# A decoder block on one core: the first weights in two parts, the compressed key's norm joined to another, 18 routing constants

## The chip, the core and the metric

The kernel runs on one core of a Trainium2 chip. A core has TensorE (PE in the rows: matmuls and transposes, with PEld for loading the stationary operand), VectorE (DVE), ScalarE (ACT), GpSimd (POOL) and SyncE (SP), which here only issues loads and stores. The metric is the device time of one execution in microseconds (us); smaller is better. The time before is the median of three runs.

## The reference

One block of a decoder for 512 tokens of width 2048 in float32. Cut to what matters here:

```python
h = rms(x, attn_norm_g);  proj = h @ w_in            # q, 6 x k/v, branch gates, pool input, merge gates
kc = rope(rms(compress(k_cmp), k_norm_cmp_g));  vc = compress(v_cmp)
    # compress: blocks of 32 tokens + position embedding, silu(flat @ w1) @ w2
q, k_slc, k_swa = rope(rms(., gain)) each
o = gate0*attend(q, kc, vc) + gate1*attend(selected blocks) + gate2*attend(window)
y = merge0 * (o @ w_head_out) + merge1 * (pool(pool_in) @ w_pool) * pool_scale
x = x + y @ w_out
p = softmax(rms(x) @ w_router_group + b), top group;  top 2 of its 4 experts
x = x + sum of the chosen experts' (silu(h @ w_gate) * (h @ w_up)) @ w_down
```

## The kernel before

Every large product is done three times over in a split form: a weight piece is loaded (`raw_*`), ScalarE casts it to its high part (`hi_*`), VectorE or GpSimd subtracts the two to get the low part (`lo_*`), and TensorE multiplies high by high, low by high and high by low (`mm3`, lines 133 to 136; `Piece.split`, lines 173 to 197). Which of the two engines subtracts is a pattern of letters for each kind of weight in `PLAN['lo']`: G is GpSimd, V VectorE, read in a circle.

`run` (line 201) walks over a list of such pieces in a fixed order. The string `PLAN['main']` sets the order of the second stage: after the eight pieces `cmp` of the compressed keys and values come two gate pieces (g, h), then pieces of the first attention group's queries, keys and values (q; q0, q2, ... q14), mixed with four pieces K0 to K3 of the compression's first weights for the keys and V0 to V3 for the values (called `w` in tile names; their product is `H`). A second string, `PLAN['side']`, is a row of slots, one taken after each part of a piece; a letter is a function that runs there, a dot an empty slot. `g` is the gate's transposes (`gate_T`, line 571), `B` and `D` build the compression's input from the transposed keys and values (`Xf`, its high part `Xh`, its low part `Xl`, lines 459 to 463), `h` and `i` transpose the hidden layer `cth` into `hsT` (line 492) and copy it with a factor (line 498), `k` makes the compressed key with its norm and rope (`cmp_key`, lines 505 to 526), `w` transposes that key (`kcT`, line 530) and makes the compressed value (`c2v`, line 537), `v` is the latter alone. The queue of each engine keeps the order in which the program records its instructions.

**The opening.** x is loaded in column pieces, transposed on TensorE (`ht`, line 402), multiplied by the norm's gain `gcol` into its high part by ScalarE (line 403) and its low part by VectorE (line 404); the first `cmp` piece is loaded, cast and subtracted whole. `gcol` itself comes from a transpose (`gcolp`, line 309).

**The first attention group's queries and keys.** When q14 is through, VectorE works along a chain (lines 618 to 642): squares, an inverse root over 24 columns, norm, gains, rope. TensorE transposes the result (`qT`, line 658). The same chain runs for groups 1 to 3, later.

**The routing.** The last product with `w_out` ends token tile by token tile; each tile is added to x, squared with a sum on ScalarE (line 1048), transposed (`xgT`, line 1081), copied by ScalarE (`xgt`, line 1083) and multiplied by the router's weights (`lgp`, line 1088). Small operations on VectorE follow (from `lg`, line 1420, to `mx`, line 1451), then a product with constants (`pref`, line 1457). In between, `warm_up` (line 1412) lets TensorE multiply constants whose result nobody reads.

Of the kernel before, what the change touches and what calls it, by code (L numbers as in the profile page):

```python
# [76 lines left out]
def hybrid_block_kernel(  # L77
# [262 lines left out]
    def late_loads():  # L340
        q = nc.sync
        for i in range(4):
            q.dma_start(gain[:, i], q_norm_g.to_broadcast([128, 64]))
        q.dma_start(gain[:, 4], k_norm_slc_g.to_broadcast([128, 64]))
        q.dma_start(gain[:, 5], k_norm_swa_g.to_broadcast([128, 64]))
# [156 lines left out]
    kc_row = early.tile([128, 64], F32, name="kc_row")  # L502
    kcd = early.tile([128, 2, 64], F32, name="kcd")

    def cmp_key():
# [11 lines left out]
        rt = early.tile([128, 4, 8], F32, name="crt")  # L517
# [1079 lines left out]
```

## Time and profile before

| | before |
|---|---|
| median of 3 runs | 1443.61 us (1442.37 to 1444.62) |
| the profiled execution | 1442.58 us, its span 1440.8 us |
| mean granted clock of TensorE | 0.984 of full |
| TensorE busy | 1388.4 us, 96% |
| VectorE busy | 825.1 us, 57% |
| ScalarE busy | 765.6 us, 53% |
| GpSimd busy | 445.4 us, 31% |

Busy shares say which engine could be the bound. The list of waits says for what an engine stood idle, and for how long; the number in square brackets at the end of a timeline row is the same for one instruction. [...]

### The profile page before, as it was taken

The page shows a single profiled execution, that of the slowest core. Times are in us where ns is not written, and L with a number is a line of the kernel's source. Part 1 is how long each engine was busy: PE and PEld are TensorE (multiplying, and loading weights), DVE is VectorE, ACT ScalarE, POOL GpSimd, SP SyncE. Part 2 cuts the span into 40 slices and gives each one's busy share as a digit, 9 for nine tenths or more (in the row PEclk, how much of TensorE's full clock was granted, in tenths as well). Part 3 has the DMA queues.
Part 4 walks back from the last instruction along what each step waited for, and adds up shares of the span by engine and source line. Part 5 has one row for each costly group of instructions (what it writes and reads, how often), then busy time and mean ns, then how long its engine had stood idle before and what let it go on. Part 6 is the DMA issues. An engine that isn't in the chain of part 4 may idle for free.

```text
span 1440.8 us, 18395 instructions
## 1 busy us (share of the span) xinstructions
PE 1388.4 (96%) x6638; PEld 1138.2 (79%) x6638; DVE 825.1 (57%) x1258; ACT 765.6 (53%) x1289; POOL 445.4 (31%) x289
## 2 busy tenths in 40 slices
PE   8998999989999999999999999999999999999995
PEld 7877788778778788788888888888887777777774
DVE  4663773666463453555543202453255899999995
ACT  4543356564666465655665322332242687777784
POOL 0044342322333343243434455211021322222221
PEclk9999999999999999999999999999999999999998
DMA  6344233233333333343434453785675899999994
GB/s 224 94 115 123 80 102 87 77 107 85 91 116 111 92 93 87 96 117 97 109 110 125 117 141 108 224 326 166 226 252 175 279 362 367 367 358 354 330 363 84
DMA packets 193188, 249.88 MB, mean 173 GB/s; under 512 B 50384, under 2 KB 137536, under 8 KB 191264
## 3 DMA queue, kind: packets, MB, share of 16 engines
q1 hardware_dynamic: 176640, 199.13, 43.6%
q0 software_dynamic: 11808, 41.09, 10.0%
q10 hardware_dynamic: 4640, 8.40, 1.6%
q8 instruction: 54, 0.88, 0.3%
q14 instruction: 46, 0.38, 0.1%
HBM read 225.49 MB, written 35.65 MB: 181 GB/s over the span
## 4 chain that ended last, share of the span: by engine, by line
PE 79%; DVE 10%; ACT 6%; issue 2%; DMA 1%; POOL 1%; ACTq 0%; SPq 0%; POOLq 0%; DVEq 0%
PE z L134 7%; PE z L136 7%; PE z L135 7%; PE gu L136 4%; PE gu L134 4%; PE gu L135 4%; PE wo L134 4%; PE wo L136 4%; PE wo L135 4%; PE qkv L135 2%; PE qkv L134 2%; PE qkv L136 2%; PE dn L134 2%; PE dn L135 2%; PE dn L136 2%; PE xT L1245 2%
## 5 line engine op out<-in xcount | busy, mean ns | idle before, releaser
L197 POOL TENSOR_TENSOR lo_z<-raw_z,hi_z 128x1024 fp32r<-128x1024 f32 x64 | 153.4, 2401 | 200.5 <-ACT hi_z L196 192.8
L134 PE MATMUL z<-hT,hi_z 128*128 128x512 f32 x512 | 204.1, 399 | 0.0
L136 PE MATMUL z<-hT,lo_z 128*128 128x512 f32 x512 | 200.7, 392 | 0.0
L135 PE MATMUL z<-hT,hi_z 128*128 128x512 f32 x512 | 200.2, 391 | 0.0
L140 DVE TENSOR_TENSOR ptl<-pt,pth 128x512 fp32r<-128x512 f32 (+1 forms) x96 | 57.8, 602 | 177.0 <-ACT pth L139 176.8
L197 DVE TENSOR_TENSOR lo_gu<-raw_gu,hi_gu 128x2048 fp32r<-128x2048 f32 x64 | 146.8, 2294 | 9.8 <-ACT hi_gu L196 4.2
L196 ACT CAST hi_gu<-raw_gu 128x2048 fp32r<-128x2048 f32 x64 | 122.3, 1911 | 18.7 <-PE gu L136 9.9
L778 ACT ACTIVATE p<-s,m 128x128 f32<-128x128 f32 (+3 forms) x128 | 66.4, 523 | 115.6 <-DVE m L776 112.4
L197 POOL TENSOR_TENSOR lo_qkv<-raw_qkv,hi_qkv 128x1024 fp32r<-128x1024 f32 x28 | 70.6, 2521 | 173.8 <-ACT hi_qkv L196 148.6
L136 PEld LDWEIGHTS z<-hT,lo_z 128*128 128x128 f32 x512 | 96.5, 189 | 21.2
L135 PEld LDWEIGHTS z<-hT,hi_z 128*128 128x128 f32 x512 | 96.7, 189 | 18.6
L134 PEld LDWEIGHTS z<-hT,hi_z 128*128 128x128 f32 x512 | 96.9, 189 | 18.3
L134 PE MATMUL gu<-hi_gu,xh 128*112 128x512 f32 x256 | 106.4, 416 | 0.1
L134 PE MATMUL qkv<-hi_qkv,hT 128*128 128x512 f32 x256 | 103.5, 404 | 0.1
L135 PE MATMUL qkv<-lo_qkv,hT 128*128 128x512 f32 x256 | 101.4, 396 | 0.3 <-POOL lo_qkv L197 0.3
L136 PE MATMUL gu<-hi_gu,xl 128*112 128x512 f32 x256 | 101.7, 397 | 0.0
L136 PE MATMUL qkv<-hi_qkv,hT 128*128 128x512 f32 x256 | 101.5, 396 | 0.0
L134 PE MATMUL wo<-hi_wo,y 128*128 128x512 f32 x256 | 101.1, 395 | 0.0
L135 PE MATMUL gu<-lo_gu,xh 128*112 128x512 f32 x256 | 100.4, 392 | 0.0
L136 PE MATMUL wo<-hi_wo,y 128*128 128x512 f32 x256 | 99.8, 390 | 0.0
L135 PE MATMUL wo<-lo_wo,y 128*128 128x512 f32 x256 | 99.7, 389 | 0.0
L1313 POOL DMA_INDIRECT out_dram<-y,idx x18 | 60.1, 3337 | 107.7 <-ACT hi_gu L196 88.6
(419 smaller groups left out, 3193.7 us busy)
## 6 DMA issues: line engine op xcount, KB each, us to landing
raw_z<-in_w_in_dram SPq DMA_DIRECT2D x128, 256.0 KB
raw_gu<-in_w_expert_gate_dram SPq DMA_DIRECT2D x59, 512.0 KB
raw_gu<-in_w_expert_up_dram SPq DMA_DIRECT2D x59, 512.0 KB
raw_dn<-in_w_expert_down_dram SPq DMA_DIRECT2D x28, 1024.0 KB
raw_wo<-in_w_out_dram SPq DMA_DIRECT2D x32, 512.0 KB
raw_qkv<-in_w_in_dram SPq DMA_DIRECT2D x32, 256.0 KB
raw_qkv<-in_w_in_dram SPq DMA_DIRECT2D x128, 64.0 KB
raw_u<-in_w_in_dram SPq DMA_DIRECT2D x16, 512.0 KB
```

The lines of the kernel that those rows point to most:

```text
L134: T.matmul(ps, ah, bh, start=start, stop=False)
L135: T.matmul(ps, ah, bl, start=False, stop=False)
L136: T.matmul(ps, al, bh, start=False, stop=stop)
L140: V.tensor_tensor(lo, src, f(hi), op=OP.subtract)
L196: A.copy(self.hi[sl], self.raw[sl])
L197: self.eng.tensor_sub(self.lo[sl], self.raw[sl], f(self.hi[sl]))
L778: A.activation(p[:, b], v[:, b], AF.Exp, bias=m[:, b:b + 1], scale=0.125, accum_out=m[:, 2 + b:3 + b])
L1245: T.transpose(pt[:, j * RS:(j + 1) * RS], self.xr[:, k0 * 128 + j:(k0 + 4) * 128:4], ident[0:RS, 0:RS])
L1313: ins = G.indirect_dma_start(out=dst, out_offset=bass.IndirectOffsetOnAxis(ap=idx, axis=0), in_=src, in_offset=None, bounds_check=n - 1, o ...
```

## The change

**Opening.** The first `cmp` piece is loaded in two halves, one for each of its two rows of 128 inputs, and cast and subtracted in two cuts. It is no longer split ahead of everything, but behind the first two x tiles, so that on ScalarE the first x tile (`hh[0]`) stands ahead of the cast; the second (`hh[1]`) is made by VectorE. The splits of the next two pieces stand behind the x tiles 2 and 3. The gain's transpose goes into a bank of the constants' tile, so the first `ht` waits for nothing that reads it. The first twelve `cmp` matmuls run as four of high by high, four of low x, four of low weight.

**Slots and engines.** `g` moves three slots on, behind q4 and K1; `i` and the compressed value one slot on; the key's transpose leaves its slot. In `PLAN['lo']` two subtractions go from GpSimd to VectorE: K1's and q6's.

**The compressed key's norm.** The two operations for its sum of squares, its inverse root and the rest, 14 on VectorE, go: ScalarE squares the key with a sum (`kc_sum`), the sum becomes a 25th column of the first group's inverse root, and scaling and rope of the key run behind that group's rope, followed by its transpose.

**Gains.** The operation with the queries' and keys' gains, one of 1536 columns, becomes one of 4 x 256 and one of 4 x 128, and the tile of gains is loaded in three parts rather than six.

**Routing.** The transposes of the last two tiles are recorded ahead of what they stood behind, and 15 constants become 18.

```diff
-    'side': 'mnab.Bcd.gD.........h.k.iw',
+    'side': 'mnab.Bcd..D.g.......h.k..iv',
-    'lo': {'qkv': 'VGVGVGVGGG...', ..., 'w': 'GGV', ...},
+    'lo': {'qkv': 'VGVVVGVGGG...', ..., 'w': 'GVVGGVGG', ...},
...
-    pc = o_tile("gcolp")
-    T.transpose(pc[:, 0:16], grow, ident[0:16, 0:16])
-    V.tensor_copy(gcol, pc[:, 0:16])
+    T.transpose(warm[:, 1, 0:16], grow, ident[0:16, 0:16])
+    V.tensor_copy(gcol, warm[:, 1, 0:16])
+    cmp[0].cuts = tuple((slice(None), slice(k, k + 1)) for k in range(2))
+    cmp0_mm = cmp[0].mm
+    def cmp0_first(wh, wl, part):
+        if part:
+            return cmp0_mm(wh, wl, part)
+        cmp0.extend(mm_tile(f"cmp_{t}") for t in range(NT))
+        for i, (a, w) in enumerate(((hh[0], wh), (hl[0], wh), (hh[0], wl))):
+            for t in range(NT):
+                T.matmul(cmp0[t], a[:, t * 128:(t + 1) * 128], w[:, 0], start=i == 0, stop=False)
+    cmp[0].mm = cmp0_first
...
-            A.mul(hh[k], ps, gcol[:, k:k + 1])
+            if k == 1:
+                V.tensor_scalar(hh[k], ps, gcol[:, k:k + 1], None, op0=OP.mult)
+            else:
+                A.mul(hh[k], ps, gcol[:, k:k + 1])
...
         A.copy(kc_row, po[:, 0:64])
-        sq = early.tile([128, 64], F32, name="csq")
-        V.tensor_mul(sq, kc_row, kc_row)
-        cs = early.tile([128, 3], F32, name="cs")
-        V.tensor_reduce(cs[:, 0:1], sq, axis=AX.X, op=OP.add)
-        V.tensor_scalar(cs[:, 0:1], cs[:, 0:1], 1.0 / HD, EPS, op0=OP.mult, op1=OP.add)
-        rsqrt(cs[:, 1:2], cs[:, 0:1], cs[:, 2:3])
-        V.scalar_tensor_tensor(kc_row, kc_row, cs[:, 1:2], gainc, op0=OP.mult, op1=OP.mult)
+        A.activation(kcd[:, 0], po[:, 0:64], AF.Square, accum_out=kc_sum)
+    def cmp_key_rope(inverse):
+        V.scalar_tensor_tensor(kc_row, kc_row, inverse, gainc, op0=OP.mult, op1=OP.mult)
...
+            if g == 0:
+                V.tensor_copy(s2[:, NT * 6:], kc_sum)
...
-                V.tensor_tensor(q3, q3, gain.rearrange("p h d -> p (h d)")[:, None, :].to_broadcast([128, NT, 384]),
+                V.tensor_tensor(qn[:, :, 0:4], qn[:, :, 0:4], gain[:, 0, None, None, :].to_broadcast([128, NT, 4, 64]),
+                                op=OP.mult)
+                V.tensor_tensor(qn[:, :, 4:6], qn[:, :, 4:6], gain[:, None, 1:3].to_broadcast([128, NT, 2, 64]),
                                 op=OP.mult)
...
+            key = [lambda: cmp_key_rope(rs[:, NT * 6:])] if g == 0 else []
+            if g == 0:
+                deferred.append(cmp_keyT)
...
-            residual_tile(3, t, ps[t])
             if t:
                 router_T(3, t - 1)
+            residual_tile(3, t, ps[t])
...
-                tl[0] += [lambda: router_mm(3, 2), lambda: router_T(3, 3), lambda: router_mm(3, 3)]
+                tl[0] += [lambda: router_T(3, 3), lambda: router_mm(3, 2), lambda: router_mm(3, 3)]
...
-    cmp[0].split()
-    run(main, side)
+    run(main, side, split_lead=lambda i: 2 if i else 0)
...
-    warm_up(15)
+    warm_up(18)
```

VectorE's queue at the second half of the compression's input, before: `gates` reads the gate's transposes, `Xf` and `Xl` belong to the values, the `lo_w` behind them is K2's.

```order
L451 COPY kT_165<-kvT_799 64x511 x2
L572 TENSOR_SCALAR gates<-gateT 128x192
L459 TENSOR_TENSOR Xf_867<-kT_165,cols 128x2048
L463 TENSOR_TENSOR Xl_870<-Xf_867,Xh_869 128x2048
L197 TENSOR_TENSOR lo_w_888<-raw_w_885,hi_w_887 128x1024
```

The same place after:

```order
L469 COPY kT_168<-kvT_799 64x511 x2
L197 TENSOR_TENSOR lo_w_823<-raw_w_820,hi_w_822 128x1024
L197 TENSOR_TENSOR lo_qkv_6_846<-raw_qkv_6_839,hi_qkv_6_845 128x1024
L477 TENSOR_TENSOR Xf_861<-kT_168,cols 128x2048
L481 TENSOR_TENSOR Xl_864<-Xf_861,Xh_863 128x2048
L197 TENSOR_TENSOR lo_w_882<-raw_w_879,hi_w_881 128x1024
L585 TENSOR_SCALAR gates<-gateT 128x192
```

The subtractions of K1 (`lo_w_823`) and q6 now stand between the last key copy and `Xf`, and `gates` stands behind K2's subtraction.

TensorE's queue at the transposes of the values' hidden layer, before: `H` is the product with V3, `hi_qkv_12` and `lo_qkv_12` are q12's weights.

```order
L134 MATMUL H_961<-hi_w_1054,Xh_869 128x256
L135 MATMUL H_961<-lo_w_1055,Xh_869 128x256
L136 MATMUL H_961<-hi_w_1054,Xl_870 128x256
L492 MATMUL hsT_1158<-ident,cth_1155 128x128 x2
L134 MATMUL qkv_0_738<-hi_qkv_12_1117,hT_88 128x512
L135 MATMUL qkv_0_738<-lo_qkv_12_1118,hT_88 128x512
```

The same transposes after, with the end of the matmuls of q12's first part ahead of them:

```order
L134 MATMUL qkv_3_741<-hi_qkv_12_1093,hT_88 128x512
L135 MATMUL qkv_3_741<-lo_qkv_12_1094,hT_88 128x512
L136 MATMUL qkv_3_741<-hi_qkv_12_1093,hT_88 128x512
L510 MATMUL hsT_1152<-ident,cth_1131 128x128 x2
L134 MATMUL qkv_0_738<-hi_qkv_12_1093,hT_88 128x512
L135 MATMUL qkv_0_738<-lo_qkv_12_1094,hT_88 128x512
```

They have moved behind the twelve matmuls of q12's first part, and `c2v`, which read their copy behind that part, now stands behind the second.

TensorE's queue at the end of the routing's products, before:

```order
L1081 MATMUL xgT_2_9057<-ident,xg_2_9021 128x128 x4
L1088 MATMUL lgp<-wr_7643,xgt_1_9032 128x20 x4
L1088 MATMUL lgp<-wr_7643,xgt_2_9062 128x20 x4
L1081 MATMUL xgT_3_9072<-ident,xg_3_9051 128x128 x4
L1088 MATMUL lgp<-wr_7643,xgt_3_9077 128x20 x4
L1412 MATMUL warm_9097<-ones 128x512 x15
```

And after:

```order
L1100 MATMUL xgT_2_9040<-ident,xg_2_9018 128x128 x4
L1107 MATMUL lgp<-wr_7633,xgt_1_9015 128x20 x4
L1100 MATMUL xgT_3_9058<-ident,xg_3_9048 128x128 x4
L1107 MATMUL lgp<-wr_7633,xgt_2_9045 128x20 x4
L1107 MATMUL lgp<-wr_7633,xgt_3_9063 128x20 x4
L1430 MATMUL warm_9087<-ones 128x512 x18
```

The transposes of tile 3 have gone ahead of the product with tile 2, and three constants are added.

## Rows read from the trace of the kernel before

**Rows 1.** The page, part 1: each engine's busy us, share of the span, instructions.
```profile
PE 1388.4 (96%) x6638; PEld 1138.2 (79%) x6638; DVE 825.1 (57%) x1258; ACT 765.6 (53%) x1289; POOL 445.4 (31%) x289
```

**Rows 2.** List of TensorE's waits: waiting instruction, releaser, us in total, times, longest.
```profile
PE qT L658 <- DVE qn L642: 2.3, 1, 2.3
...
PE lgp L1088 <- ACT xgt L1083: 1.5, 2, 0.8
```

**Rows 3.** Timeline, opening: start, us, engine, line, operation, count, idle before and its releaser.
```profile
7.67 1.04 ACT L196 CAST hi_cmp<-raw_cmp 128x1024 fp32r<-128x1024 f32 x1 [4.91 <-DMA raw_cmp<-in_w_in_dram]
...
8.62 1.26 ACT L403 ACTIVATE hT<-ht,gcol 128x512 fp32r<-128x512 f32 x2
...
9.36 0.50 PE L134 MATMUL cmp<-hi_cmp,hT 128*128 128x512 f32 x1 [2.15 <-ACT hT L403]
...
9.89 1.40 DVE L404 SCALAR_TENSOR_TENSOR hT<-ht,gcol,hT 128x512 fp32r<-128x512 f32 x2
...
14.36 1.04 PE L402 MATMUL ht<-ident,xt 128*128 128x128 f32 x8
```

**Rows 4.** Stretch of the opening: busy time by engine, granted clock, DMA share, GB/s.
```profile
11.00:13.00 2.00, 2.00 (x6) 1.52 (x6) 1.52 (x2) 0.69 (x1) 0.00 (x0) 0.50 1.04 378
```

**Rows 5.** Timeline, gate to weight piece K2: TensorE, VectorE, GpSimd, ScalarE.
```profile
73.41 3.71 DVE L459 TENSOR_TENSOR Xf<-kT,cols 128x2048 f32<-128x2048 f32 x1
...
87.12 0.42 PE L571 MATMUL gateT<-ident,gt 48*128 48x48 f32 x4 [1.87 <-DVE kT L451]
...
87.85 5.37 DVE L459 TENSOR_TENSOR Xf<-kT,cols 128x2048 f32<-128x2048 f32 x1
...
88.08 1.05 ACT L196 CAST hi_qkv<-raw_qkv 128x1024 fp32r<-128x1024 f32 x1 [0.88 <-DMA raw_qkv<-in_w_in_dram]
...
96.10 0.40 PE L134 MATMUL qkv<-hi_qkv,hT 128*128 128x512 f32 x1
...
97.47 2.39 POOL L197 TENSOR_TENSOR lo_w<-raw_w,hi_w 128x1024 fp32r<-128x1024 f32 x1 [2.01 <-ACT hi_w L196]
...
97.53 3.42 DVE L197 TENSOR_TENSOR lo_w<-raw_w,hi_w 128x1024 fp32r<-128x1024 f32 x1
...
101.57 0.28 PE L134 MATMUL H<-hi_w,Xh 128*128 128x256 f32 x1
```

**Rows 6.** Stretch behind the gate's transposes, columns as in rows 4.
```profile
89.00:91.00 2.00, 2.00 (x6) 1.58 (x5) 2.00 (x1) 0.12 (x1) 2.00 (x2) 0.50 0.47 141
```

**Rows 7.** Timeline, compressed key and value: GpSimd, VectorE, TensorE, ScalarE.
```profile
122.21 2.34 POOL L197 TENSOR_TENSOR lo_qkv<-raw_qkv,hi_qkv 128x1024 fp32r<-128x1024 f32 x1 [3.47 <-ACT hi_qkv L196]
...
122.28 2.28 DVE L130 SCALAR_TENSOR_TENSOR cs<-cs 128x1 f32<-128x1 f32 x1
...
126.12 1.22 DVE L197 TENSOR_TENSOR lo_qkv<-raw_qkv,hi_qkv 128x1024 fp32r<-128x1024 f32 x1
...
127.73 0.69 PE L492 MATMUL hsT<-ident,cth 128*128 128x128 f32 x2 [5.38 <-DVE cth L481]
...
129.38 1.04 ACT L196 CAST hi_u<-raw_u 128x1024 fp32r<-128x1024 f32 x1
...
133.80 2.00 PE L537 MATMUL c2v<-w2v,hsTv 128*128 128x64 f32 x16 [0.38 <-DVE kcT L531]
```

**Rows 8.** Stretch behind `hsT`, columns as in rows 4.
```profile
127.00:132.00 5.00, 4.26 (x11) 3.46 (x12) 0.68 (x2) 1.96 (x2) 1.51 (x1) 0.50 0.51 151
```

**Rows 9.** The gains' line 629: times, least, median and longest ns, starts, forms.
```profile
L629 DVE TENSOR_TENSOR qn<-qn,gain x4: 1747/1754/3826, 156.9 to 614.2; 128x1536 f32<-128x1536 f32 x4
```

**Rows 10.** Timeline, routing: the constants, the choice's last operation, the prefix sums.
```profile
1107.43 6.04 PE L1412 MATMUL warm<-ones 128*128 128x512 f32 x15
...
1111.38 0.22 DVE L1451 TENSOR_TENSOR mx<-gs,top 128x64 fp32r<-128x64 f32 x1
...
1113.31 0.20 PE L1457 MATMUL pref<-mx,tri 128*128 128x80 f32 x1
```

**Rows 11.** Stretch of the routing constants, columns as in rows 4.
```profile
1106.00:1112.00 6.00, 6.00 (x19) 5.03 (x19) 3.89 (x25) 0.21 (x1) 0.00 (x0) 0.50 0.91 334
```

More of the change, by code (lines that the diff above doesn't have):

```diff
@@ L282, in hybrid_block_kernel @@
     invb = mix.tile([128, S], F32, name="invb")
-    rtmp = mix.tile([128, 24], F32, name="rtmp")
+    rtmp = mix.tile([128, 25], F32, name="rtmp")
+    kc_row = mix.tile([128, 64], F32, name="kc_row")
+    kcd = mix.tile([128, 2, 64], F32, name="kcd")
+    kc_sum = mix.tile([128, 1], F32, name="kc_sum")
+    gainc = mix.tile([128, 64], F32, name="gainc")
     gates = mix.tile([128, NT, 48], F32, name="gates")
@@ L295, in hybrid_block_kernel @@
     nc.scalar.dma_start(grow, attn_norm_g.rearrange("o (k p) -> (o k) p", p=128))
-    cmp = token_major("cmp", lambda raw, k0: [(raw, wcols(k0, 2, C_KC, 512))], hh, hl, lambda ps: cmp_done(ps), one=(KT - 2,),
+    cmp0 = []
+    cmp = token_major("cmp", lambda raw, k0: [(raw[:, k:k + 1], wcols(k0 + k, 1, C_KC, 512)) for k in range(2)]
+                      if k0 == 0 else [(raw, wcols(k0, 2, C_KC, 512))], hh, hl, lambda ps: cmp_done(ps), one=(KT - 2,), out=cmp0,
                       pre={4: lambda: load_x(2, 4), 8: lambda: load_x(4, 6),
@@ L320, in hybrid_block_kernel @@
     sc = mix.tile([128, 5, 2, 8], F32, name="sincos")
-    gain = mix.tile([128, 6, 64], F32, name="gain")
+    gain = mix.tile([128, 3, 64], F32, name="gain")
     posi = early.tile([128, 5], I32, name="posi")
-    gainc = early.tile([128, 64], F32, name="gainc")
     w2k = early.tile([128, 2, 64], F32, name="w2k")
@@ L341, in late_loads @@
         q = nc.sync
[L342 to L345, printed above, removed]
+        for i, g_ in enumerate((q_norm_g, k_norm_slc_g, k_norm_swa_g)):
+            q.dma_start(gain[:, i], g_.to_broadcast([128, 64]))
         q.dma_start(gainc, k_norm_cmp_g.to_broadcast([128, 64]))
@@ L500, in cmp_hidT @@
         HT[i] = hsT
-    kc_row = early.tile([128, 64], F32, name="kc_row")
-    kcd = early.tile([128, 2, 64], F32, name="kcd")
     def cmp_key():
@@ L509, in cmp_key @@
         A.copy(kc_row, po[:, 0:64])
[L510 to L517 removed]
+        A.activation(kcd[:, 0], po[:, 0:64], AF.Square, accum_out=kc_sum)
+    def cmp_key_rope(inverse):
+        V.scalar_tensor_tensor(kc_row, kc_row, inverse, gainc, op0=OP.mult, op1=OP.mult)
+        rt = pools["att"].tile([128, 4, 8], F32, tag="pe", name="crt")
         x1, x2 = kc_row[:, 0:8], kc_row[:, 8:16]
@@ L602, in done @@
             vt = VT[g] = att.tile([128, NT, 2, 128], F32R, tag="vt", name=f"vt{g}", bufs=2)
-            ss = att.tile([128, 2, NT, 6], F32, tag="ss", name=f"ss{g}")
+            ss = att.tile([128, 2, NT * 6 + 1], F32, tag="ss", name=f"ss{g}")
             for t in range(NT):
@@ L642, in rope @@
                 V.tensor_add(x2, rt[:, 2], rt[:, 3])
-            deferred.extend([lambda: squares(0), lambda: squares(1), inverse, norm, gains, rope,
-                             lambda: marks.add(f"qkv{g}")])
+            key = [lambda: cmp_key_rope(rs[:, NT * 6:])] if g == 0 else []
+            deferred.extend([lambda: squares(0), lambda: squares(1), inverse, norm, gains,
+                             lambda: [fn() for fn in [rope] + key], lambda: marks.add(f"qkv{g}")])
+            if g == 0:
+                deferred.append(cmp_keyT)
         return token_major(f"qkv{g}", loads, hh, hl, done, eng=G)
```

9 lines of the change are left out of this document (4 added, 5 removed), and 2 rows, old and new, of the table PLAN.

## The prediction

> **What bounds the kernel now.** I read the page first: TensorE is busy for 1388.4 of 1440.8 us, and no other engine is above 57% [rows 1]. So time can only come out of the some 52 us in which TensorE stands idle, and out of stretches in which its matmuls run at the lower clock; work taken off another engine counts only where TensorE waits for it. Second came the list of what TensorE waits for [rows 2], and from it the few waits that the change is near: the first weights in the opening [rows 3], the gate's transposes [rows 5], the compressed value's transposes `hsT` [rows 7], the queries' transposes `qT` and the last logits `lgp` [rows 2]. Third, the granted clock by stretch. [...] The price of those: 24 matmuls of 512 columns take 101.57 - 96.10 = 5.47 us at full clock, 0.228 each [rows 5]; of the 133.80 - 127.73 = 6.07 us from `hsT` to `c2v`, in a stretch at 0.50, the twelve matmuls between them take some 5.1 (1.0 for three transposes) instead of 2.7 [rows 7, 8]. So one matmul costs 0.2 us more at the lower clock.
>
> The sum is made against the profiled execution, 1442.58 us. It lies 1.0 below the median, so I add 1.0 at the end. All that stands behind the routing, and what lies between the places below, I let shift as it is: its loads are issued when a buffer comes free, so they move with TensorE.
>
> **Opening: 3.0 us gained.** Before, ScalarE casts the whole first weight piece when it has landed at 7.67 (1.04 us), only then makes the normalised x (two of 0.63), and TensorE starts at 9.36 after an idle of 2.15 [rows 3]. Now the first x is scaled ahead of the cast, and the cast needs only half a piece, 1.04/2 = 0.5 us. A half cannot be cast earlier than about 7.0 (the whole lands at 7.67), so the first matmul comes at 7.6 to 7.8: 1.7 gained. The second part is the stream behind it. The first twelve matmuls take 9.36 to 14.36, 5.00 us [rows 3], mostly at half clock [rows 4]; at full clock 12 x 0.228 = 2.7. VectorE now has to make four pieces before the low weights are there, the two low parts of x (0.70 each [rows 3]), the second x and half a subtraction, some 0.7 each: from 6.9 to 9.7. The twelve then end at about 10.6 rather than 14.36, and the eight transposes behind them (1.04) at 11.7. What is late next is the second weight piece: its subtraction now stands behind the x parts of the next two tiles, and is done at about 14.9, when TensorE wants it at 14.4, so 0.4 is given back. 14.36 - 10.6 - 0.4 = 3.3; I take 3.0. Low end 1.2, if the clock falls at about 10 as before and only the earlier start is left; high end 3.5.
>
> **Gate and weight piece K2: 2.0 us lost.** The four gate transposes waited 1.87 us for VectorE's key copies [rows 5] and the clock was at 0.50 behind them [rows 6]: eight matmuls more slowly by 0.2 are 1.6. Moved behind q4 and K1 they find their tile free. So TensorE would reach K2 at 101.57 - 1.87 - 1.6 = 98.1. But two subtractions, of K1 and of q6, go from GpSimd to VectorE and stand there ahead of `Xf`, with `Xl` and K2's own subtraction behind it. Each costs 1.22 alone [rows 7]. The second cannot start before ScalarE's cast of 88.08 + 1.05 = 89.13 [rows 5], so it ends at 90.4, and `Xf` starts there instead of at 87.85. `Xf` took 5.37 us while GpSimd ran its subtractions, and 3.71 with GpSimd idle [rows 5], as it is now: it ends at 94.1 instead of 93.2. From its end to the end of K2's subtraction before are 100.95 - 93.22 = 7.7 us, which hold a cast, `Xl`, and 3.42 us for a subtraction that takes 1.22 alone, because GpSimd's V0 began at 97.47 and this one at 97.53 [rows 5]. That chain keeps its order, so K2's low weights come at 101.8. TensorE, there at 98.1, waits 3.7 us, starts K2 0.25 later than before, and then runs at the lower clock: the price behind the gate was 1.6 and behind `hsT` 2.3; I take 1.75. Net -2.0; -4 if the clock takes longer; +2.0 if VectorE goes first (below).
>
> The rows show the two engines taking turns, a whole instruction each. [...]
>
> **Compressed key's norm, `hsT`: 7.9 us gained.** This is the largest term. `hsT` waited 5.38 us for `cth` on VectorE, behind the key's chain of 14 small operations, one of which took 2.28 us while GpSimd's subtraction ran beside it, and behind a subtraction of 1.22 [rows 7]. The 14 leave the path; one square with a sum on ScalarE (about 0.25) takes their place, and the rest of the key's work runs behind the first group's rope. The subtraction for q12 then comes at about 121 to 122.3, just before TensorE is through with V3, and `cth` at 123.2. `hsT` itself stands twelve matmuls later, so there is room of nearly 2 us. Gained are 5.38, the slow clock of those twelve (5.1 - 2.7 = 2.3), and 0.4 for the key's transpose between `hsT` and `c2v`; 0.2 off for a short wait. The key's eight operations of 1.2 us in all and its transpose fall into VectorE's wait for ScalarE behind `qT`; were that cover gone, they would cost 1.2. What is late next: ScalarE now casts `hi_u` ahead of the copy that `c2v` needs (third case). Range 5.5 to 8.5.
>
> **Queries: 0.3 and 0.2 lost.** The 2.28 us wait at `qT` [rows 2] is for a VectorE chain, and that grows by a copy of one column (0.15) and by a second gains operation: one of 1536 columns took 1.75 in three groups [rows 9]; as 1024 and 512 I price 1.2 + 0.7. It took 3.83 in the first group, with GpSimd beside it; another meeting there can give -1.5 or +0.5. Groups 1 to 3 may lose 0.2 together. Three loads of gains fewer on the load queue save nothing: nobody waits for that queue there.
>
> **Routing: 2.3 us gained.** TensorE waited 1.5 us in two pieces for ScalarE's copies [rows 2]; with the last transposes ahead of `lgp(2)` and the copy ahead of the square, about 0.3 is left, and `lgp(3)` ends near 1105.3. The logits' chain on VectorE ends with `mx` at 1111.38 + 0.22 [rows 10]; it starts when `lgp` and the norm's inverse are there, now about 1105.9 rather than 1107.63, so `mx` is there at 1109.9. `pref` started only at 1113.31 because the 15 constants, 6.04 us at half clock, held TensorE [rows 10, 11]. 18 constants at full clock are 18 x 0.228 = 4.1, ending at 1109.4, and `pref` follows at 1110: 3.3. At half clock they take 7.7, end near 1113, and 0.3 to 0.5 is left; three constants more, 3 x 0.43 = 1.3, against nothing gained, is the low end of -0.8. With 0.3 us of waits instead of 1.5 I lean to the full clock, but matmuls of 20 columns still stand there: 2.3.
>
> **Sum.** 3.0 - 2.0 + 7.9 - 0.3 - 0.2 + 2.3 = 10.7; 1442.58 - 10.7 + 1.0 = 1432.9.
>
> **The rivals.** First, **K2 is not late**: VectorE's subtraction starts before GpSimd's V0, or they do not meet, and K2's weights are there at 99.6. Then TensorE waits 1.5 us, begins K2 2.0 earlier than before, and no long slow stretch follows; the term is +2.0 instead of -2.0: 1428.9. For it: only 0.06 us separated the two [rows 5]. Against: ScalarE's casts of both keep their distance from `Xl`. Chance 0.15.
>
> Second, **the clock falls in the opening and at the routing as before**. Then these give 1.6 and 0.5 instead of 3.0 and 2.3: 10.7 - 1.4 - 1.8 = 7.5, so 1436.1. For it: TensorE still has a broken stretch of transposes and short matmuls at both places. Chance 0.22. [...] No row here separates transposes from the idle beside them.
>
> Third, **the change does not do what it says: the wait moves from `hsT` to `c2v`**. ScalarE's copy of `hsT` now stands behind the cast of `hi_u`, which waits for its load. That had landed by 129.38 at the latest, when the cast began [rows 7]; so the copy could end as late as 131.4, while TensorE wants `c2v` at 128.1. 3.3 us and a slow stretch of 2: 1438.2. Against: the cast did not wait before. Chance 0.08; together with the second case it comes near no change.
>
> Fourth, **slower**: the idle at K2, the longest that is left, keeps the clock down. The point from which it decides: 10.7 us are eaten by 54 matmuls at 0.2 us, a slow stretch of 23 us beyond the one that I have counted, and 1446.6, 13.7 us later, takes 69 and 29 us. The longest stretches in the trace are some 6 us [rows 8, 11]. Chance 0.015.
>
> **How the numbers follow.** The forecast has 0.47, and 0.07 is left for sums of small misses. The range takes in the first three, 1428 to 1438, which leaves out the third case's far side, the fourth and the tails. About 0.2% (2.9 us) is what a measurement of this kernel can tell from no change; faster by more means under 1440.7. All but the second and third case together and the fourth lie there: 0.955 faster, 0.03 the same, 0.015 slower.
>
> **What the profile of the changed kernel would show.** Right: first matmul of `cmp` before 8, and second piece's at about 15; a wait at `H` for `lo_w` of 3 to 4 us near 95 to 100, with GpSimd's V0 running in it; no wait at `hsT` and full clock behind it; a wait at `qT` as long as before; `pref` within 9.5 us of the last `wo` matmul. Wrong: a wait of over 1 us at `c2v`, none at K2, or a clock of 0.50 in the opening and around the 18 constants.

## The result and the profile after

The changed kernel takes 1434.32 us (median of 3, 1433.58 to 1434.72) against 1443.61 us; the ratio is 0.9935 [0.9913, 0.9958]. Its profiled execution took 1434.72 us with a span of 1432.9, so 7.9 us of span are to be accounted for. I forecast 1432.9 us. Direction and range held. The sum was 10.7, 2.8 more than the two profiled executions show; the medians lie 9.3 apart.

The ledger below is made from the start of the same matmul in both profiles: how much earlier it starts after the change, place by place. The differences between neighbouring places are what each place gave or took.

| place | start before | start after | gained there | forecast |
|---|---|---|---|---|
| opening, up to the first of K0 | 83.59 | 80.78 | +2.8 | +3.0 |
| gate, K1, K2, up to the first of q8 | 104.41 | 103.39 | -1.8 | -2.0 |
| `hsT`, `c2v`, up to the first of q14 | 138.45 | 128.67 | +8.8 | +7.9 |
| queries of group 0, behind `qT` | | | -0.3 | -0.3 |
| queries of groups 1 to 3 | | | -2.3 | -0.2 |
| stretches at the lower clock near 362 and 482, drift | | | -1.2 | 0 |
| last `wo` matmul | 1101.01 | 1095.07 | (5.9 in all) | |
| routing, up to `pref` | 1113.31 | 1105.08 | +2.3 | +2.3 |
| first expert and tail | | | -0.4 | 0 |

So all terms but one came out within 0.9 us. That one is wrong by 2.1, and some 1.6 us went at places that the prediction let shift as they were.

The page's first part (columns as in [rows 1]) and TensorE's waits (columns as in [rows 2]):

```profile
PE 1386.4 (97%) x6641; PEld 1136.2 (79%) x6641; DVE 823.3 (57%) x1253; ACT 764.9 (53%) x1291; POOL 435.0 (30%) x287
```

```profile
PE pt L816 <- ACT p L806: 6.4, 3, 2.7
...
PE H L135 <- DVE lo_w L197: 3.6, 1, 3.6
...
PE qT L677 <- DVE qn L658: 2.4, 1, 2.4
```

Against [rows 1] TensorE is busy 2.0 us less and the span is 7.9 shorter: the rest, 5.9, is idle time that went. `qT` waits as long as before [rows 2], `lgp` is no longer in the list, one wait is new, that of `H` for `lo_w`, and within the line of `pt` one of 0.39 has become one of 2.65 (rows below).

**Opening.** Timeline of the first microseconds and the stretch that answers to [rows 4]:

```profile
7.75 2.11 PE L326 MATMUL cmp<-hi_cmp,hT 128*128 128x512 f32 x8 [0.56 <-ACT hi_cmp L196]
...
11.11 1.04 PE L417 MATMUL ht<-ident,xt 128*128 128x128 f32 x8
```

```profile
11.00:13.00 2.00, 2.00 (x15) 1.75 (x14) 0.53 (x1) 1.25 (x3) 0.00 (x0) 1.00 1.03 389
```

The first matmul starts at 7.75 instead of 9.36, the second eight transposes at 11.11 instead of 14.36 [rows 3], and the granted clock of 11 to 13 is 1.00 of full where it was 0.50 [rows 4].

**Gate and K2.** Timeline and the stretch behind K2's wait, to be laid beside [rows 5]:

```profile
86.60 1.23 DVE L197 TENSOR_TENSOR lo_qkv<-raw_qkv,hi_qkv 128x1024 fp32r<-128x1024 f32 x1 [0.94 <-ACT hi_qkv L196]
...
87.75 3.72 DVE L477 TENSOR_TENSOR Xf<-kT,cols 128x2048 f32<-128x2048 f32 x1
...
95.23 0.28 PE L134 MATMUL H<-hi_w,Xh 128*128 128x256 f32 x1
...
95.44 2.50 POOL L197 TENSOR_TENSOR lo_w<-raw_w,hi_w 128x1024 fp32r<-128x1024 f32 x1 [14.32 <-ACT hi_w L196]
...
95.65 3.37 DVE L197 TENSOR_TENSOR lo_w<-raw_w,hi_w 128x1024 fp32r<-128x1024 f32 x1
...
99.07 0.58 PE L135 MATMUL H<-lo_w,Xh 128*128 128x256 f32 x1 [3.56 <-DVE lo_w L197]
```

```profile
100.00:102.00 2.00, 2.00 (x11) 2.00 (x10) 0.54 (x1) 0.00 (x0) 0.00 (x0) 0.50 1.05 367
```

TensorE reaches K2 at 95.23 and stops at the second matmul for 3.56 us. K2's subtraction on VectorE started 0.21 us after GpSimd's V0 and took 3.37 instead of 1.22. Behind the wait the clock is 0.50 until about 102.5, and 1.00 from there. The gate's transposes, which waited 1.87 before, wait for nothing.

**Compressed value.** Timeline and the stretch behind `hsT`, to be laid beside [rows 7, 8]:

```profile
120.01 1.23 DVE L197 TENSOR_TENSOR lo_qkv<-raw_qkv,hi_qkv 128x1024 fp32r<-128x1024 f32 x1 [8.68 <-PE H L136]
...
121.82 0.42 DVE L499 SCALAR_TENSOR_TENSOR cth<-cth,H 128x256 f32<-128x256 f32 x1 [0.59 <-ACT cth L498]
...
123.98 0.38 PE L510 MATMUL hsT<-ident,cth 128*128 128x128 f32 x2
...
126.97 1.89 PE L550 MATMUL c2v<-w2v,hsTv 128*128 128x64 f32 x16
```

```profile
124.00:128.00 4.00, 4.00 (x25) 3.48 (x24) 0.00 (x0) 1.86 (x2) 1.99 (x1) 1.00 0.73 198
```

Neither `hsT` nor `c2v` has a wait behind its line, and the clock is 1.00. `cth` ends at 122.24, 1.7 us before `hsT` starts.

**Routing and first expert.** Timeline of the last transposes, the constants and the prefix sums, beside [rows 10], and two stretches:

```profile
1097.07 0.63 PE L1100 MATMUL xgT<-ident,xg 128*128 128x128 f32 x4 [0.36 <-DVE xg L1062]
...
1099.39 5.86 PE L1430 MATMUL warm<-ones 128*128 128x512 f32 x18
...
1103.58 0.23 DVE L1469 TENSOR_TENSOR mx<-gs,top 128x64 fp32r<-128x64 f32 x1
...
1105.08 0.20 PE L1475 MATMUL pref<-mx,tri 128*128 128x80 f32 x1
```

```profile
1100.00:1102.00 2.00, 2.00 (x6) 1.62 (x5) 1.69 (x11) 0.22 (x1) 0.00 (x0) 0.50 1.01 317
...
1113.00:1116.00 3.00, 2.92 (x8) 1.98 (x8) 1.17 (x2) 0.66 (x2) 2.27 (x4) 0.50 0.25 46
```

Two waits of 0.83 and 0.68 us for ScalarE's copies have become one of 0.36 for VectorE. `mx` is there at 1103.81, but `pref` starts at 1105.08, because the 18 constants, partly at 0.50, hold TensorE 1.3 us longer (5.86 us for the 18, the clock 0.50 at 1100 to 1102).

**What was not forecast: queries of group 1.** Timeline of the gains after:

```profile
268.04 1.23 DVE L643 TENSOR_TENSOR qn<-qn,gain 128x1024 f32<-128x1024 f32 x1
...
268.90 2.62 POOL L197 TENSOR_TENSOR lo_wp<-raw_wp,hi_wp 128x1024 fp32r<-128x1024 f32 x1 [7.12 <-ACT hi_wp L196]
...
269.18 2.89 DVE L645 TENSOR_TENSOR qn<-qn,gain 128x512 f32<-128x512 f32 x1
...
272.82 0.17 DVE L802 RECIPROCAL m<-m 128x2 f32<-128x2 f32 x1
...
274.45 0.33 PE L816 MATMUL pt<-ident,p 128*128 128x128 f32 x1 [2.65 <-ACT p L806]
```

and the same operations before:

```profile
277.44 1.76 DVE L629 TENSOR_TENSOR qn<-qn,gain 128x1536 f32<-128x1536 f32 x1
...
278.31 3.15 POOL L197 TENSOR_TENSOR lo_wp<-raw_wp,hi_wp 128x1024 fp32r<-128x1024 f32 x1 [7.12 <-ACT hi_wp L196]
...
279.95 0.17 DVE L783 RECIPROCAL m<-m 128x2 f32<-128x2 f32 x1
...
280.03 1.64 DVE L637 TENSOR_TENSOR rt<-qn,sincos 128x192 f32<-128x192 f32 x1
...
281.58 0.33 PE L797 MATMUL pt<-ident,p 128*128 128x128 f32 x1 [0.39 <-ACT p L787]
```

Before, GpSimd's subtraction `lo_wp` had its data at 278.31, while the one gains operation ran, and took 3.15 us, to 281.46; the time that VectorE lost beside it fell on the first rope operation (1.64 instead of 0.35), behind the reciprocal that TensorE needs through `p`. After, `lo_wp` starts at 268.90, near the end of the first gains operation, and the second, of 512 columns, takes 2.89 instead of 0.68 (the median of the four groups). The reciprocal stands behind it, and `pt` waits 2.65 instead of 0.39.

**And near 362.** The waiting matmul and the stretch behind it, after and then before:

```profile
362.16 0.80 PE L788 MATMUL s<-k,q 128*128 128x512 f32 x1 [2.48 <-ACT p L797]
```

```profile
362.00:365.00 3.00, 2.84 (x7) 2.26 (x8) 0.86 (x3) 2.43 (x7) 1.88 (x1) 0.50 0.00 0
```

```profile
369.19 0.50 PE L769 MATMUL s<-k,q 128*128 128x512 f32 x1 [2.57 <-ACT p L778]
```

```profile
369.00:373.00 4.00, 3.81 (x17) 3.12 (x18) 2.26 (x4) 2.79 (x8) 2.40 (x1) 1.00 0.00 0
```

TensorE idles as long at this place in both (2.48 and 2.57 us). Behind it the clock is 0.50 after and 1.00 before; that costs 1.4 us. At about 482 it is the other way round (a stretch of 3.4 us at 0.50 instead of one of 6.8), which gives 0.9 back.

### The profile page after: what moved, and what is told of

It reads as the page before. It is cut to its first block, busy times and chain, and to the rows that moved or that the text cites. A ratio compares the mean times of both kernels' runs of the same rounds, so it can differ in the third digit from the quotient of the medians.

```text
span 1432.9 us, 18389 instructions
## 1 busy us (share of the span) xinstructions
PE 1386.4 (97%) x6641; PEld 1136.2 (79%) x6641; DVE 823.3 (57%) x1253; ACT 764.9 (53%) x1291; POOL 435.0 (30%) x287
## 4 chain that ended last, share of the span: by engine, by line
PE 81%; DVE 10%; ACT 5%; issue 2%; POOL 1%; DMA 0%; ACTq 0%; SPq 0%; POOLq 0%; DVEq 0%
PE z L136 7%; PE z L135 7%; PE z L134 7%; PE gu L136 4%; PE gu L134 4%; PE gu L135 4%; PE wo L134 4%; PE wo L136 4%; PE wo L135 4%; PE qkv L135 3%; PE qkv L136 3%; PE qkv L134 3%; PE o L831 2%; PE dn L134 2%; PE dn L135 2%; PE pt L816 2%
## 5 line engine op out<-in xcount | busy, mean ns | idle before, releaser
L197 POOL TENSOR_TENSOR lo_qkv<-raw_qkv,hi_qkv 128x1024 fp32r<-128x1024 f32 x27 | 64.8, 2402 | 174.9 <-ACT hi_qkv L196 149.2
```

The source lines that it names most:

```text
L197: self.eng.tensor_sub(self.lo[sl], self.raw[sl], f(self.hi[sl]))
```

## The experiments

Unless said otherwise each is an edit of the changed kernel. The kernel before, timed in the same three groups of runs, had medians of 1442.91, 1442.31 and 1442.78 us; ratios are to it.

### The two gains operations in the other order

```diff
-                V.tensor_tensor(qn[:, :, 0:4], qn[:, :, 0:4], gain[:, 0, None, None, :].to_broadcast([128, NT, 4, 64]),
-                                op=OP.mult)
                 V.tensor_tensor(qn[:, :, 4:6], qn[:, :, 4:6], gain[:, None, 1:3].to_broadcast([128, NT, 2, 64]),
                                 op=OP.mult)
+                V.tensor_tensor(qn[:, :, 0:4], qn[:, :, 0:4], gain[:, 0, None, None, :].to_broadcast([128, NT, 4, 64]),
+                                op=OP.mult)
```

> The changed kernel with its two gains operations in the other order: the one of 4 x 128 columns first, the one of 4 x 256 behind it, in all four groups. Theory (a gap for GpSimd): in group 1 GpSimd's subtraction lo_wp became ready at 268.90, during the first of the two operations, and ran in the gap between them, so that the second took 2.89 us and TensorE waited 2.65 us at pt instead of 0.39. With the long one second, lo_wp becomes ready during the second one, has to wait for its end, and the delay falls on the first rope operation, behind the division that pt needs, as in the kernel before. Expected: the wait of TensorE at that pt back at 0.4 us, the offset there 2.2 us better than in the changed kernel, the time near 1432. Rival (the second operation costs by itself, or the wait comes from elsewhere): the wait stays at 2.5 to 2.7 and the time at 1434.3.

1430.22 us, 0.9923 [0.9901, 0.9946], span 1427.8. Timeline of group 1:

```profile
266.56 0.69 DVE L643 TENSOR_TENSOR qn<-qn,gain 128x512 f32<-128x512 f32 x1
...
267.17 1.22 DVE L645 TENSOR_TENSOR qn<-qn,gain 128x1024 f32<-128x1024 f32 x1
...
267.43 3.21 POOL L197 TENSOR_TENSOR lo_wp<-raw_wp,hi_wp 128x1024 fp32r<-128x1024 f32 x1 [7.12 <-ACT hi_wp L196]
...
269.22 1.63 DVE L653 TENSOR_TENSOR rt<-qn,sincos 128x192 f32<-128x192 f32 x1
...
270.77 0.33 PE L816 MATMUL pt<-ident,p 128*128 128x128 f32 x1 [0.45 <-ACT p L806]
```

The work is the same. Now `lo_wp` becomes ready at 267.43, when the gap between the two operations is past and the long one runs; the operation beside it that takes longer is again the first of the rope (1.63 instead of 0.34), behind the reciprocal, as before the change. `pt` waits 0.45 instead of 2.65. So the split itself is harmless; what costs 2.2 us is its gap at the moment when GpSimd stands ready, ahead of an operation that then takes 2.89 us (0.69 here). This is shown for group 1. The span fell by 5.1, more than the 2.2: in this execution the routing's 18 constants took 4.37 us instead of 5.86, of which more below; where the rest came from no row here shows.

### Who subtracts q6, and who K2

```diff
-    'lo': {'qkv': 'VGVVVGVGGG...', ...},
+    'lo': {'qkv': 'VGVGVGVGGG...', ...},
```

> The changed kernel with q6's subtraction back on GpSimd; K1's stays on VectorE. Theory (VectorE's queue ahead of Xf makes K2 late, since q6's cast ends only at 86.57): Xf starts at 85.7 instead of 87.75, K2's subtraction ends near 97.7 instead of 99.0, and TensorE's wait of 3.6 us at K2 shrinks to under 0.5; but GpSimd's subtraction for q6 has to wait for Xf's end at 89.4, and TensorE waits for it 1.5 to 2.5 us at q6. Net 0.5 to 2 us better at the end of K2, and up to 1.6 more if the clock stays up. Rival (K2 is late only because GpSimd's subtraction of V0 goes first): the wait at K2 stays at 2.5 us or more, and the time is that of the changed kernel or worse.

1429.79 us, 0.9909 [0.9892, 0.9925]. K2 waits for nothing; q6 now waits 1.40 for GpSimd, and the clock is 0.50 behind it (93 to 96). Timeline of VectorE, with the wait:

```profile
85.59 3.75 DVE L477 TENSOR_TENSOR Xf<-kT,cols 128x2048 f32<-128x2048 f32 x1
...
91.57 0.50 PE L135 MATMUL qkv<-lo_qkv,hT 128*128 128x512 f32 x1 [1.40 <-POOL lo_qkv L197]
...
93.59 3.39 DVE L197 TENSOR_TENSOR lo_w<-raw_w,hi_w 128x1024 fp32r<-128x1024 f32 x1
```

`Xf` starts 2.2 us sooner without q6's subtraction ahead of it, and the whole chain to K2's low weights, still with the same meeting (3.39), moves as much: the low weights are there at 96.98 instead of 99.02. TensorE, held up at q6, comes to K2 only at 98.53 instead of 95.23. The gain by q12 is 2.0 us. So 2.0 of the 3.56 us at K2 came from q6's subtraction ahead of `Xf`, as the prediction's second term has it; the rest, the meeting with V0's subtraction, is still there and is covered here by TensorE's later arrival. K1's subtraction stayed where the change has it, so its share is not shown. The profiled execution is the longest of the four (1432.25 us); against the changed kernel it is 2.5 us better, and the medians lie 4.5 apart; where the other runs gained more no trace shows.

```diff
-    'lo': {..., 'w': 'GVVGGVGG', ...},
+    'lo': {..., 'w': 'GVGVGVGG', ...},
```

> The changed kernel with K2's subtraction on GpSimd and V0's on VectorE, the two exchanged. [...]

1432.43 us, 0.9926 [0.9909, 0.9942]. K2 on GpSimd and V0 on VectorE: the wait is 2.91 instead of 3.56. In the profile after, `Xl` ends at 95.73, and a subtraction on GpSimd took 2.39 [rows 5]: if VectorE's queue up to `Xl` sets the time, K2's low weights come at 98.1 and the wait is 2.7, by estimate. If the meeting with V0 were the whole cost, 3.56 - 2.39 = 1.2 would be left. 2.91 is near the first. The clock did not follow the wait: at 100 to 102 it is 1.00 here, behind 2.91, and 0.50 in the kernel after, behind 3.56. Of the 2.0 us gained by q12, some 1.2 are that.

### 15 constants

```diff
-    warm_up(18)
+    warm_up(15)
```

> The changed kernel with 15 constants at the routing instead of 18. The choice's last operation ended at 1103.8 and the prefix sums began at 1105.08, behind the last constant, the clock having come back near 1102.6. Theory (the reordered transposes give the gain, the three constants cost): the prefix sums begin 0.6 to 0.7 us sooner after the last wo matmul, the slow stretch there stays as long, 0.7 us better in all. Rival (the constants are needed to bring the clock back): with fewer of them the clock comes back later or falls again in the first expert, and the time is the same or up to 2 us worse.

1433.13 us, 0.9936 [0.9919, 0.9953]. `pref` comes 1.1 us sooner and waits 0.99 for the choice. But the constants ran faster in this execution (15 in 3.69 us, 0.25 each, instead of 18 in 5.86, 0.33 each), and in the first experiment, with 18, they did too (4.37 us, 0.24 each), with `pref` 1.1 sooner. So the run does not tell fewer constants from a better clock: inconclusive. What can be read is that at this pace TensorE waits for the choice with 18 as well (0.31), and then the number decides nothing; the routing's order alone, below, says more.

### The value's slot one earlier

```diff
-    'side': 'mnab.Bcd..D.g.......h.k..iv',
+    'side': 'mnab.Bcd..D.g.......h.k.iv',
```

> The changed kernel with the values' hidden layer transposed and the compressed value made one slot earlier again, where the kernel before has them; the key's norm stays joined to the first group's. Theory (the 14 operations were the wait): VectorE has cth at 122.2 and TensorE is through with V3 near 121.4, so hsT waits 0.8 to 1.2 us instead of 5.4, c2v waits for nothing, and the stage gives 7 to 8 us instead of 8.8; 0.8 to 1 us worse than the changed kernel, up to 2.5 if the clock falls behind that wait. Rival (the slot is what removed the wait): hsT waits over 3 us and the time goes back by 5 us or more.

1436.59 us, 0.9956 [0.9943, 0.9969].

```profile
122.43 0.44 PE L510 MATMUL hsT<-ident,cth 128*128 128x128 f32 x2 [0.93 <-DVE cth L499]
```

`hsT` twelve matmuls earlier waits 0.93 for `cth`, done at 122.37, where it waited 5.38 before the change [rows 7]. The slot gives 1.3 us at q14, the key's chain the rest. That the key's chain on VectorE was the wait is shown. It is more than the 14 operations that are gone: in the kernel before, the key's scaling and rope, eight more, stood between them and q12's subtraction (119.84 to 124.76 for the 14, up to 126.05 for the eight), and these moved behind the first group's rope. No run takes one without the other.

### The moved slots alone, on the kernel before

```diff
-    'side': 'mnab.Bcd.gD.........h.k.iw',
+    'side': 'mnab.Bcd..D.g.......h.k..iw',
```

> The kernel before with the new slots of the side string alone (gate's transposes three slots on, hsT and the key's transpose with the compressed value one slot on); the key's norm, the subtractions, the opening and the routing stay as before. Theory (slots alone do little, VectorE's queue sets the time): the gate's wait of 1.87 us goes, but K2's subtraction still ends at 100.9, so TensorE waits there about 2.5 us and gains 0.5 at most; q12's subtraction stands behind the key's 14 operations and ends at 127.3, so TensorE waits some 5 us for it instead of for hsT. In all 0 to 2 us better than before, 1441 to 1443. Rival (the slots are what gains): no wait over 1.5 us between 85 and 135, and 8 us or more better, 1434 to 1436.

1445.71 us, 1.0024 [1.0014, 1.0034]: slower, which was not expected. Timeline and the stretches:

```profile
87.72 3.75 DVE L459 TENSOR_TENSOR Xf<-kT,cols 128x2048 f32<-128x2048 f32 x1
...
87.98 5.66 POOL L197 TENSOR_TENSOR lo_w<-raw_w,hi_w 128x1024 fp32r<-128x1024 f32 x1 [3.41 <-issue]
...
93.69 0.58 PE L135 MATMUL H<-lo_w,Xh 128*128 128x256 f32 x1 [2.19 <-POOL lo_w L197]
```

```profile
94.00:103.00 9.00, 8.66 (x28) 6.77 (x28) 5.45 (x3) 1.40 (x2) 6.56 (x2) 0.50 0.50 134
```

`Xf` (87.72 to 91.47) now starts 0.26 us before K1's subtraction on GpSimd, and that takes 5.66 us, to 93.64; in the kernel before, 0.52 us ahead of `Xf`, it took 2.39. K1 waits 2.19, and the clock is 0.50 for nine microseconds, 94 to 103, longer than any of the stretches in [rows 4, 6, 8, 11]. In the changed kernel K1's subtraction is on VectorE and ends at 85.66, before `Xf` starts at 87.75, so this meeting cannot come about: moving it was no free addition but belongs to the slots. That is argued; no run has the slots with that subtraction alone. The wait of q12's low weights was right in kind, but they came 6.9 us late instead of 5.

### The opening alone, on the kernel before

```diff
-    cmp[0].split()
-    run(main, side)
+    run(main, side, split_lead=lambda i: 2 if i else 0)
```

with the opening's other lines (first weights in two parts, `cmp0_first`, the gain's transpose in the constants' bank, the second x on VectorE).

> The kernel before with the new opening alone. Theory: 2.8 us better at the first matmul of weight piece K0, at full clock up to 14, all of it kept up to the gate, and the end 2.8 better, within the 1.5 us by which the slow stretches differ between executions: 1440. Rival (a gain in the opening is lost again where the loads or the waits behind it decide): the gain at K0 is under 1.5, or shrinks by over 1 us up to the wait at hsT, and the time is within 1 us of before.

1440.45 us, 0.9983 [0.9973, 0.9993]. By K0 it is 3.4 to 3.8 us ahead, and it stays so through `hsT` and `qT`. Then some 0.8 go near 327 and 1.6 near 368: 2 are left. Near 368 the clock is 0.74 (365 to 369) and 0.83 (369 to 373), and the kernel before has 1.00 in both; for 327 no row here shows it. What the opening gains is real, but with the same instructions the matmuls near 368 ran more slowly here.

### The routing's order alone, on the kernel before

```diff
-            residual_tile(3, t, ps[t])
             if t:
                 router_T(3, t - 1)
+            residual_tile(3, t, ps[t])
...
-                tl[0] += [lambda: router_mm(3, 2), lambda: router_T(3, 3), lambda: router_mm(3, 3)]
+                tl[0] += [lambda: router_T(3, 3), lambda: router_mm(3, 2), lambda: router_mm(3, 3)]
```

> The kernel before with the new order of the routing's last transposes alone, still 15 constants. Theory (the order gives the gain): ScalarE's copies are no longer waited for, the logits' products end about 1.8 us sooner after the last wo matmul, and the prefix sums begin 2 to 3.4 us sooner than before, by what the clock does there. 1440 to 1442. Rival (the three constants are needed for the gain): under 1 us sooner.

1440.25 us, 0.9985 [0.9976, 0.9995]. The first constant, behind the last logits, starts 2.4 us sooner (1105.00 instead of 1107.43) and `pref` 3.2, with 15 constants; 0.2 of both lies ahead of the routing. So the order gives the gain, and the three more constants are not needed for it. They cost something: `pref` comes 9.31 us behind the last `wo` matmul here and 10.01 in the changed kernel, with one stretch at the lower clock within the constants in both (0.57 at 1105 to 1109 here, 0.50 at 1100 to 1102 there). Of the 0.7 between, 0.1 lies ahead of the constants; the rest is about what three of them take at full clock, 3 x 0.228. Some 1.3 us go again in the first expert, where the clock of 1119 to 1122 is 0.52 and was 1.00 before.

### The joined norm alone, on the kernel before

```diff
+        A.activation(kcd[:, 0], po[:, 0:64], AF.Square, accum_out=kc_sum)
...
+            key = [lambda: cmp_key_rope(rs[:, NT * 6:])] if g == 0 else []
```

with the gains in two operations, and slots and subtractions as before, but for `v` in the place of `w`.

> The kernel before with the key's norm joined to the first group's and the gains in two operations; slots, subtractions, opening, routing and constants as before, only the key's transpose is no longer in the slot of the compressed value. Theory (the 14 operations were the wait): cth is ready 4 to 5 us sooner, hsT waits 0.5 to 1.3 us instead of 5.4, c2v for nothing; 6 to 8 us better behind c2v, of which the gap between the two gains operations gives back 2.3 in group 1: 1436 to 1440. Rival (the slots and subtractions are needed for it): hsT or q12's subtraction still keeps TensorE waiting 3 us or more, and the gain is under 3 us.

1437.65 us, 0.996 [0.9946, 0.9974].

```profile
124.35 0.59 PE L493 MATMUL hsT<-ident,cth 128*128 128x128 f32 x2 [1.88 <-DVE cth L482]
```

`hsT` waits 1.88 instead of 5.38, more than the 0.5 to 1.3 that was expected: ScalarE casts q14's weights (122.51, 1.04 us) ahead of `cth`. The gain by `c2v` is 4.8 instead of 6 to 8, since the matmuls are still slow behind that wait: the next of 512 columns start 0.43 us apart up to 127.73, and some 0.23 apart from 128.04. In group 1 `pt` waits 2.62 and the 2.3 us are lost again, which confirms the first experiment from the other side: the split of the gains does it without the slots, the subtractions or the opening. These are readings of the profiled execution, 1442.03 us, the longest of the five and 4.4 above their median: 2.4 us are left behind `pt`, and most of that goes again in slower matmuls, which start 0.43 us apart instead of 0.23, near 325 (323.8 to 325.5), 369 (367.5 to 370.1) and in the first expert (1121.2 to 1124.5). How the others came to 1435.5 to 1437.7 no trace shows.

### The parts put right, together

The other order of the gains, q6 on GpSimd and 15 constants, in one kernel:

> The changed kernel with the gains in the other order, q6's subtraction back on GpSimd, and 15 constants. If the three causes are separate places on TensorE's path, the gains add: 2.2 from the wait at pt, 1.8 from K2, and 0 to 1.2 at the routing (what the three constants cost where the clock is low). Expected 1428 to 1431, by the theory; if one of them only moved a wait to another of the three, 1432 or more.

1427.95 us, 0.9894 [0.9877, 0.991]. At their places the two gains add: 2.0 us by q12 and 2.2 more at `pt`. (The medians do not add: 4.1 and 4.5 us alone, 6.4 together.) And with q8 ahead of K2 instead of q6 on GpSimd:

```diff
-    'main': 'ghqqKqKqKVqKVqVVq',
+    'main': 'ghqqKqKqqKVKVqVVq',
```

> The changed kernel with the gains in the other order and 15 constants, and with q8 put ahead of K2 and V0 in the order of pieces; the subtractions stay as the change has them. Theory (K2 is late by VectorE's queue, so work that is ready before it can fill the wait): q8's subtraction now stands where K2's stood, behind Xl, and meets no GpSimd subtraction, so it ends at 96.9, TensorE waits 1.2 to 1.8 us for it instead of 3.6, and K2 waits for nothing. 2 us better there than in the changed kernel, about as the version with q6's subtraction on GpSimd: 1427 to 1430. Rival (what follows is then late in turn): a wait of over 2 us at K2, V0 or K3, and 1431 or more.

1426.28 us (1425.6 to 1426.76), 0.9883 [0.9867, 0.99], the best of all. K2 waits for nothing, because q8's 24 matmuls run while its low weights are made. q8 itself waits, with full clock behind it:

```profile
96.73 0.50 PE L135 MATMUL qkv<-lo_qkv,hT 128*128 128x512 f32 x1 [1.38 <-DVE lo_qkv L197]
```

```profile
98.00:100.00 2.00, 2.00 (x10) 1.69 (x9) 2.00 (x1) 0.00 (x0) 0.92 (x1) 1.00 0.64 221
```

### The changed kernel once more, without an edit

> The changed kernel once more, without an edit. Theory (the slow stretches are no part of the edits and lie elsewhere in another execution): the waits of the other profile come again within 0.3 us each, K2 3.5 to 4, pt 2.6, qT 2.4, and the time is within 1.5 us of 1434.3; the places where the clock is low differ at one or more of them, among them the routing. Rival (the clock follows from the kernel's order alone): the same low stretches at the same places, and the offsets along the kernel agree within 0.3 us throughout.

1433.35 us, 0.9932 [0.9916, 0.9949]. The waits are the same within 0.3 us (K2 3.8, `pt` 2.7, `qT` 2.4). The clock is not. Two stretches of this execution, then one of the first (1100 to 1102 of the first is shown above):

```profile
410.00:413.00 3.00, 3.00 (x9) 2.35 (x8) 2.20 (x8) 1.29 (x5) 0.00 (x0) 0.50 1.14 344
...
1100.00:1102.00 2.00, 2.00 (x12) 1.73 (x12) 1.57 (x9) 0.15 (x1) 0.00 (x0) 1.00 0.99 240
```

```profile
410.00:413.00 3.00, 2.48 (x14) 1.80 (x13) 2.25 (x7) 1.35 (x5) 0.00 (x0) 1.00 1.12 345
```

At 410 this one has 0.50 and the first 1.00; at 1100 it is the reverse. The last wait ahead is the same in both executions, 2.11 us near 408 and 0.36 near 1098. They differ by up to 1.9 us at one place of the program and by 0.2 in the span. So a single stretch at the lower clock is partly chance of the execution, and a difference of 1 to 2 us between two profiles at one place is not evidence for an edit unless a wait changed there.

## Why the prediction was right, and where it was wrong

**Opening, right.** 2.8 of 3.0. First matmul 7.75 (forecast 7.6 to 7.8), the twelve through at 11.1 (10.6), the second piece held up at 15.26 (14.9). The second rival put the lower clock here; the row says 1.00. Eight transposes start at 5.36 and eight at 11.11, and the clock is 1.00 throughout 5 to 13. No run separates transposes from the idle beside them.

**K2, right, by its working.** Forecast: `Xf` ends at 94.1, TensorE at K2 at 98.1, low weights at 101.8, a wait of 3.7. With the opening's gain of 3.0 taken off these are 91.1, 95.1, 98.8; measured 91.47, 95.23, 99.02 and 3.56. The step that decided, who goes first of K2 and V0, was left to 0.06 us in [rows 5]; it was 0.21 after the change, on GpSimd's side. By 3.37 against 1.22 alone it is worth some 2.1 us of the wait; no run turns it round, so the first rival was not put to the test. The meetings measured here are: on VectorE 3.42 before (1.22 and most of GpSimd's 2.39 [rows 5]), 3.37 after and 3.39 with q6 on GpSimd, for a subtraction of 1.22 alone, and 2.89 for a gains operation of 0.68; on GpSimd 5.66 for a subtraction of 2.39. The price of 1.75 for the slow matmuls behind K2 held in kind: 0.50 at 100 to 102.

**`hsT`, right; a size off.** 8.8 instead of 7.9. The subtraction came at 120.01 (forecast 121, less the offset of 1.0) and `cth` at 122.24 (123.2). By the starts in the two traces the 8.8 are 5.38 for the wait, 2.3 for the twelve matmuls (5.07 us against 2.77), 0.66 for the key's transpose with the wait behind it, 0.2 for `hsT` itself (0.34 against 0.13), and 0.2 in small parts. So the 0.2 for a short wait was not needed, the key's transpose was priced 0.3 too low, and `hsT` at the lower clock had no price. The third rival, `c2v` late behind ScalarE's cast of `hi_u`, is false: the cast ran before `hsT`, at 122.20.

**Queries, wrong.** The failed step is the term of -0.2 for groups 1 to 3. It priced the two gains operations as 1.2 + 0.7 in each group, saw the meeting with GpSimd for the first group alone, where [rows 9] show it as a longest time of 3826 ns, and took the median of 1754 ns to mean that the other groups have none. They have: in group 1 it lay on the next operation but two. The row gave the duration of one line; what was needed was which GpSimd instruction stands ready at the point where the new gap opens, and what waits behind it on VectorE. -2.3 was measured; two experiments show the cause.

**"Let shift as it is", partly wrong.** Between the queries and the routing nothing was edited, and yet some 1.2 us net went there, and 1.1 in the first expert against 0.7 that came back at the tail. At 362 the wait is the same (2.48 and 2.57 us), the clock behind it is not (0.50 and 1.00); in the first expert the clock is 0.50 at 1113 to 1116. The prediction had no term and no width for this. Nor is the clock low behind each longer wait: in the kernel before it was 1.00 behind 2.57 us at 369, and with K2's subtraction on GpSimd behind 2.91. Its fourth rival took the longest slow stretch to be 6 us, and the experiment with the slots alone had 9.

**Routing, right in sum, for mixed reasons.** 2.3 of 2.3: the wait shrank as forecast, and the clock was low for half of the constants (0.50 at 1100 to 1102), which the second rival had forecast for all. In the repeated execution it was 1.00 there. So that the 2.3, set between 3.3 at full clock and 0.3 to 0.5 at the lower one, came out to the tenth is luck. The sign that I named, `pref` within 9.5 us of the last `wo` matmul, was missed by 0.5 in the first execution and met in the repeated one (8.88).

Put together: 2.8 - 1.8 + 8.8 - 0.3 - 2.3 + 2.3 = 9.5 for the terms against 10.7; 1.2 and 0.4 lost elsewhere leave 7.9. That the forecast of 1432.9 us lies only 1.4 from the median is partly luck: the profiled execution before lies 1.0 below its median and the one after 0.4 above, and the misses at `hsT` (+0.9) and at the queries (-2.1) have opposite signs.

## What to carry to other kernels

Before one VectorE operation is made into two, look which GpSimd instruction stands ready at that moment and who waits for what comes behind on VectorE (here the second operation took 2.89 us instead of 0.68, and TensorE waited 2.65); put the gap where GpSimd has nothing ready, or behind the result that another engine needs. Where moved work makes a weight piece late, look for a piece that is ready and can change places with it: with that, the other order of the gains and 15 constants, 1426.28 us were reached here. And do not read one slow-clock stretch as an effect of an edit when the wait ahead of it is the same; profile the same kernel twice first.

## What the runs showed of the hardware that I had not expected

- An operation of VectorE that takes 0.68 us alone took 2.89 when a GpSimd subtraction that stood ready began 0.28 us before it; with the same two operations in the other order neither was stretched in group 1 (0.69 and 1.22).
- A wait of 2.5 us was followed by a granted clock of 0.50 in one kernel and of 1.00 in another (362 and 369 us), and the same program showed 0.50 and 1.00 at the same place in two executions (410 and 1100 us).
- Behind a wait of 2.19 us the clock was 0.50 for nine microseconds (94 to 103), behind one of 3.56 it was back at 1.00 by 103.
